# Two neighbouring seven-product pairs in the down projection give way to single ones

## The chip, the cores and the metric

The kernel runs on one core of a Trainium2 chip. The metric is the device time of one execution in microseconds (us). Engines are named as in the profile: PE does matmuls, PEld the weight loads beside them, DVE elementwise work, ACT casts, copies and activations, POOL a few small things, and SP issues the transfers of the weights.

## The reference

One decoder layer on 256 tokens of width 2048, all float32. Cut to what matters here:

```python
h = rmsnorm(x, pre_mlp_g[l])
f = jnp.square(jax.nn.relu(h @ w_up[l])) @ w_down[l]     # 2048 -> 8192 -> 2048
x = x + rmsnorm(f, post_mlp_g[l])
```

Ahead of it stands the token mixing: an input projection, four mixers, and a merge under sigmoid gates whose logits are `z = h @ w_in[l]`. The gate part of that projection (2048 rows, 8192 columns) is computed in the same way as the down projection, and it serves as a comparison below.

## The kernel before

**Three matmuls for one product.** Every float32 matrix is split into a part `hi` of few bits and a remainder `lo`. A product of a 128x128 block of activations with a 128x512 block of weights is three matmuls: hi by hi, hi by lo, lo by hi (lines 808, 809, 810 in `eight_sums`). A weight tile arrives by a 1 MB transfer as `raw`, 128 rows of 2048 numbers (three buffers). `w_emit` takes it in pieces of at most 1024 columns: ACT casts the piece to `hi` (line 102), DVE subtracts to get `lo` (line 103). There are four buffers of `hi` and four of `lo`, so the cast of a piece waits until PE is done with the piece four before it.

**Calls and pairs.** The hidden width of 8192 is worked off in four quarters `q`. In each, the up projection fills `fx` (16 blocks of 128 hidden channels by 256 tokens), and then `eight_sums` multiplies it with w_down: two calls a quarter, one for each half of the output columns, but only one call in the last quarter (its other half goes through `chunk_nat` as tile `dn`). That is seven calls. A call goes through eight pairs `p` of row blocks, 0 to 7. A pair is one `raw` tile: 2x2 blocks of weights against 2x2 blocks of activations.

**Seven or eight products.** A pair outside of `SEVEN` takes eight block products, 24 matmuls, from two pieces of weights. A pair in `SEVEN` takes a scheme with seven, 21 matmuls, at the price of sums and differences on both sides. On the side of the weights `seven(raw)` makes them in place, in four pieces that hang on each other:

```python
def first():      # after the cast and the remainder of piece 1
    V.tensor_tensor(b4[:, :, 0], b4[:, 1], b4[:, :, 0], ALU.subtract)          # line 161
def second():     # after those of piece 2
    V.tensor_tensor(b4[:, 1, 1], b4[:, 1, 1], b4[:, 0, 0], ALU.subtract)       # line 164
    V.tensor_tensor(b4[:, 0, 1], b4[:, 0, 1], b4[:, 1, 1], ALU.subtract)       # line 165
return [(b4[:, 0], first), (b4[:, 1, 1], second), (b4[:, :, 0], None), (b4[:, :, 1], None)]
```

Pieces 1, 3 and 4 have 1024 columns, piece 2 has 512. PE uses the pieces in this order for 6, 3, 6 and 6 matmuls. On the side of the activations, `keep_sums` writes four 128x128 sums for every pair of `SEVEN` into `sx`, during the up projection.

**Results.** Eight PSUM banks M1 to M8 add up over the call. M1, M5, M6 and M7 take products of seven-product pairs alone, so they are complete in the last such pair, which is pair 5. `evac` copies a finished bank to `acc` on ACT in the first quarter (line 1164) and adds it there on DVE in the others (line 1166).

**The gate projection.** It has six calls of the same `eight_sums` with `SEVEN_G = (1, 3, 5)`, on tiles of the same size from w_g, and another evacuation (`evac_g`: M1 and M5 are copied on ACT, sums on DVE follow).

The order of instructions on each engine is fixed when the program is built. It isn't always that of the code: a ready matmul may be put ahead of one whose operand was expected later.

Of the kernel before, what the change touches and what calls it, by code (L numbers as in the profile page):

```python
# [32 lines left out]
QK_SCALE = 192 ** -0.5  # L33
TWO_PI = 6.283185307179586

SEVEN = (1, 2, 4, 5)
SEVEN_G = (1, 3, 5)


# [35 lines left out]
def trunk(ctx: ExitStack, tc: tile.TileContext, t: dict):  # L75
# [16 lines left out]
    def w2(name):  # L92
        return sm.tile([P, 512], F32, tag="w2", name=name, bufs=5)
# [7 lines left out]
    def split(src, hi, lo):  # L101
        a = A.copy(hi, src)  # L102
        return a, V.tensor_tensor(lo, src, hi.bitcast(F32), ALU.subtract)  # L103


    def w_items():
# [30 lines left out]
        for q in range(NQ):  # L137
# [5 lines left out]
            for h in range(2 if q < NQ - 1 else 1):  # L143
                for p in range(8):
                    yield (t["w_down"].rearrange("(r c g) p n -> r g p c n", c=2, g=4)[
                        q * 2 + h, p // 2, :, :, p % 2 * HC:(p % 2 + 1) * HC], PC, "seven" if p in SEVEN else "eight")
            if q == NQ - 1:
# [99 lines left out]
    def small(name, n=1):  # L247
        return cst.tile([P, n], F32, name=name)
# [520 lines left out]
    def sums(ue, uo):  # L769

        s = w2("s")
        s1, s3, s_2, s4 = (s[:, o * P:(o + 1) * P] for o in range(4))
        V.tensor_tensor(s1, ue[:, P:], uo[:, P:], ALU.add)
        V.tensor_tensor(s3, ue[:, :P], ue[:, P:], ALU.subtract)
        V.tensor_tensor(s_2, s1, ue[:, :P], ALU.subtract)
        V.tensor_tensor(s4, uo[:, :P], s_2, ALU.subtract)
        return s

    def eight_sums(xs, sx, which, evac):

        def row(k, i):
            return tuple(xs[:, k, a, i * P:(i + 1) * P] for a in range(2))

        def products():
            for p in range(8):
                a11, a21, a12, a22 = row(2 * p, 0), row(2 * p, 1), row(2 * p + 1, 0), row(2 * p + 1, 1)
                if p in which:
                    u1, u3, u2, u4 = (sx(which.index(p), o) for o in range(4))
                    yield (M1, a11, 0), (M2, a12, 512)
                    yield (M3, u4, 0),  # L790
                    yield (M7, u3, 512), (M5, u1, 0)
                    yield (M4, a22, 0), (M6, u2, 512)
                else:
                    yield (M2, a11, 0), (M2, a12, 512), (M4, a21, 0), (M4, a22, 512)
                    yield (M3, a11, 0), (M3, a12, 512), (M8, a21, 0), (M8, a22, 512)
        pieces = list(products())
        left = [sum(m[0] == b for piece in pieces for m in piece) for b in range(8)]
        ps = [None] * 8
        for piece in pieces:
            hi, lo = w_get()  # L800
            due, late[:] = list(late), []
            for b, (xh, xl), off in piece:
                first = ps[b] is None
                if first:
                    ps[b] = (bank if b < 4 else aux)("sum")
                left[b] -= 1
                wh, wl = hi[:, off:off + 512], lo[:, off:off + 512]
                T.matmul(ps[b], xh, wh, start=first, stop=False)  # L808
                T.matmul(ps[b], xh, wl, start=False, stop=False)  # L809
                T.matmul(ps[b], xl, wh, start=False, stop=not left[b])  # L810
                if not left[b]:
                    late.append(lambda b=b: evac(b, ps))
            for e in due:
                e()
            tick()
# [262 lines left out]
    def keep_sums(p, ue, uo):  # L1078
        i = SEVEN.index(p)
        split(sums(ue, uo), sx[:, i, 0], sx[:, i, 1])  # L1080

    def first_hidden(fx):
# [7 lines left out]
        for c in range(0, 4, 2):  # L1090
# [4 lines left out]
            split(tp.rearrange("p (e s) -> p e s", e=2), fx[:, c:c + 2, 0], fx[:, c:c + 2, 1])  # L1095
            if c // 2 in SEVEN:
                uc = w2("uc")
# [7 lines left out]
    xr = mp.tile([P, NT, D], F32, tag="og", name="xr")  # L1105
    sx = mp.tile([P, len(SEVEN), 2, 512], F32R, tag="xg", name="sx")
    fst = [small(f"fst{i}", 4) for i in range(NT)]
# [30 lines left out]
    for q in range(NQ):  # L1138
# [7 lines left out]
        for b in range(4 if q == 0 else 0, KQ):  # L1146
# [5 lines left out]
            split(u, fx[:, b, 0], fx[:, b, 1])  # L1152
            if b // 2 in SEVEN:
                if b % 2:
# [7 lines left out]
        def evac(h, b, ps):  # L1162
            if q == 0:
                A.copy(acc[h][:, b], ps[b])
            else:
                V.tensor_tensor(acc[h][:, b], ps[b], acc[h][:, b], ALU.add)

        for h in range(2 if q < NQ - 1 else 1):
            eight_sums(fx, lambda i, o: tuple(sx[:, i, a, o * P:(o + 1) * P] for a in range(2)), SEVEN,
                       lambda b, ps, h=h: evac(h, b, ps))  # L1170
# [135 lines left out]
```

## Time and profile before

| what | value |
|---|---|
| median of 3 runs | 1502.41 us (1500.91 to 1505.73) |
| the profiled execution's own time | 1501.62 us |
| its span, first to last instruction | 1499.9 us |
| mean granted TensorE clock | 0.996 |
| PE busy | 1472.8 us (98%) |
| PEld busy | 1236.3 us (82%) |
| DVE busy | 1205.1 us (80%) |
| ACT busy | 800.8 us (53%) |

Busy matmuls overlap each other in this profile (one of 512 columns lasts about 0.39 us, and the next starts before it ends), so the pace of PE is read from starts, not from durations. Rows of the windows give the stretch, its length, the busy time and count of PE, PEld, DVE, ACT and POOL, the granted clock (1.00 is full), the busy share of the DMA engines and GB/s. Rows of the timeline give the start, the duration of the group, and in brackets the idle time of the engine ahead of it.

### The profile page before, as it was taken

The numbers are of one execution on the slowest core, as the hardware profiler recorded it, in microseconds if no ns is written. First come the engines' busy times: TensorE is split into PE (matmuls) and PEld (weight loads), VectorE is DVE, ScalarE is ACT, GpSimd is POOL, SyncE is SP. The second block draws the span as 40 slices with busy tenths as digits, with TensorE's granted clock in tenths as the row PEclk, the third lists the DMA queues.
The fourth block names the chain that finished last, engine by engine and source line by source line (L and its number), as shares of the span: only waits on it lengthen the run. The fifth ranks groups of instructions, "written<-read, shape, count | busy, mean of one in ns | idle before, by whom it ended". The sixth has DMA issues, their size and how long they took to land.

```text
span 1499.9 us, 18735 instructions
## 1 busy us (share of the span) xinstructions
PE 1472.8 (98%) x7192; PEld 1236.3 (82%) x7192; DVE 1205.1 (80%) x1697; ACT 800.8 (53%) x1078; POOL 20.0 (1%) x36
## 2 busy tenths in 40 slices
PE   9999999999999999999999999999999999999997
PEld 7988888888888888888878887888778887788875
DVE  6878788977798798796668888777997779987886
ACT  6655655445555555554445656655554545555552
POOL 0100000000000000000000000000000000000000
PEclk9999999999999999999999999999999999999999
DMA  8655544544655655656656645655556545655563
GB/s 268 219 192 173 180 171 153 187 172 167 226 200 172 226 203 170 226 203 241 245 213 253 216 164 200 213 194 194 169 171 227 194 166 199 210 184 196 168 253 113
DMA packets 57113, 295.76 MB, mean 197 GB/s; under 512 B 5120, under 2 KB 5248, under 8 KB 36544
## 3 DMA queue, kind: packets, MB, share of 16 engines
q1 hardware_dynamic: 55072, 280.68, 53.7%
q0 software_dynamic: 1952, 13.89, 2.6%
q8 instruction: 56, 0.92, 0.2%
q14 instruction: 33, 0.27, 0.1%
HBM read 290.36 MB, written 4.19 MB: 196 GB/s over the span
## 4 chain that ended last, share of the span: by engine, by line
PE 90%; DVE 5%; ACT 2%; issue 1%; DMA 1%; POOL 0%; POOLq 0%; ACTq 0%; SPq 0%; DVEq 0%
PE up L216 15%; PE sum L810 10%; PE sum L809 10%; PE sum L808 10%; PE up L219 8%; PE yb L205 2%; PE yb L206 2%; PE yb L207 2%; ACT hi L102 2%; DVE lo L103 2%; PE zg L205 2%; PE zg L207 2%; PE zg L206 2%; PE o L206 2%; PE o L205 2%; PE o L207 2%
## 5 line engine op out<-in xcount | busy, mean ns | idle before, releaser
L102 ACT CAST hi<-raw 128x1024 fp32r<-128x1024 f32 (+3 forms) x624 | 621.3, 1012 | 461.0 <-PE sum L810 112.3
L103 DVE TENSOR_TENSOR lo<-raw,hi 128x1024 fp32r<-128x1024 f32 (+3 forms) x624 | 720.9, 1173 | 168.3 <-ACT hi L102 160.8
L216 PE MATMUL up<-h,hi 128*128 128x512 f32 x960 | 229.9, 391 | 0.0
L216 PEld LDWEIGHTS up<-h,hi 128*128 128x128 f32 x960 | 176.3, 188 | 34.1
L808 PE MATMUL sum<-hi,fx 128*128 128x512 f32 x308 | 121.6, 395 | 12.3 <-ACT hi L102 12.3
L219 PEld LDWEIGHTS up<-h,lo 128*128 128x128 f32 x960 | 123.1, 191 | 4.7
L219 PE MATMUL up<-h,lo 128*128 128x256 f32 x960 | 124.8, 283 | 0.0
L809 PE MATMUL sum<-lo,hx 128*128 128x512 f32 x312 | 121.4, 389 | 0.0
L810 PE MATMUL sum<-hi,hx 128*128 128x512 f32 x312 | 121.4, 389 | 0.0
L808 PE MATMUL sum<-hi,hx 128*128 128x512 f32 x312 | 121.4, 389 | 0.0
L809 PE MATMUL sum<-lo,fx 128*128 128x512 f32 x308 | 120.0, 390 | 0.0
L810 PE MATMUL sum<-hi,fx 128*128 128x512 f32 x308 | 119.9, 389 | 0.0
L244 ACT COPY jn<-up 128x256 f32<-128x256 f32 x60 | 22.4, 372 | 115.3 <-PE up L216 115.3
L808 PEld LDWEIGHTS sum<-hi,fx 128*128 128x128 f32 x308 | 57.8, 188 | 30.3 <-ACT hi L102 18.4
L245 DVE TENSOR_TENSOR u<-up,jn 128x256 f32<-128x256 f32 x60 | 25.4, 424 | 65.0 <-ACT jn L244 65.0
L809 PEld LDWEIGHTS sum<-lo,hx 128*128 128x128 f32 x312 | 58.6, 188 | 12.3
L810 PEld LDWEIGHTS sum<-hi,hx 128*128 128x128 f32 x312 | 58.6, 188 | 12.2
L808 PEld LDWEIGHTS sum<-hi,hx 128*128 128x128 f32 x312 | 58.6, 188 | 12.2
L810 PEld LDWEIGHTS sum<-hi,fx 128*128 128x128 f32 x308 | 57.8, 188 | 12.3
L809 PEld LDWEIGHTS sum<-lo,fx 128*128 128x128 f32 x308 | 57.8, 188 | 12.2
L161 DVE TENSOR_TENSOR raw<-raw 128x1024 f32<-128x1024 f32 x46 | 56.0, 1218 | 0.2
L500 DVE SCALAR_TENSOR_TENSOR cy<-glu,consts,cy 128x253 f32<-128x253 f32 (+15 forms) x120 | 55.3, 463 | 0.6
(409 smaller groups left out, 2400.1 us busy)
## 6 DMA issues: line engine op xcount, KB each, us to landing
raw<-in_w_g SPq DMA_DIRECT2D x64, 1024.0 KB, 5.5
raw<-in_w_up SPq DMA_DIRECT2D x64, 1024.0 KB, 4.9
raw<-in_w_down SPq DMA_DIRECT2D x64, 1024.0 KB, 5.5
raw<-in_w_out SPq DMA_DIRECT2D x16, 1024.0 KB, 4.9
raw<-in_attn_proj SPq DMA_DIRECT2D x8, 1024.0 KB, 4.9
raw<-in_w_ca SPq DMA_DIRECT2D x4, 1024.0 KB, 4.9
raw<-in_w_cg SPq DMA_DIRECT2D x4, 1024.0 KB, 5.1
raw<-in_w_sv SPq DMA_DIRECT2D x4, 1024.0 KB, 4.8
```

The costliest lines, as they stand in the source:

```text
L102: a = A.copy(hi, src)
L103: return a, V.tensor_tensor(lo, src, hi.bitcast(F32), ALU.subtract)
L161: V.tensor_tensor(b4[:, :, 0], b4[:, 1], b4[:, :, 0], ALU.subtract)
L205: T.matmul(o, xh, wh, start=first, stop=False)
L206: T.matmul(o, xh, wl, start=False, stop=False)
L207: T.matmul(o, xl, wh, start=False, stop=last)
L216: T.matmul(ps, w[0][:, off:off + P], xs[:, k].rearrange("p a s -> p (a s)"), start=first, stop=last)
L219: T.matmul(ps[:, :S], w[1][:, off:off + P], xs[:, k, 0], start=False, stop=False)
L500: V.scalar_tensor_tensor(y, glu[:, b, :S - w], c, y, ALU.mult, ALU.add)
L808: T.matmul(ps[b], xh, wh, start=first, stop=False)
L809: T.matmul(ps[b], xh, wl, start=False, stop=False)
L810: T.matmul(ps[b], xl, wh, start=False, stop=not left[b])
```

## The change

One constant. The pairs of the down projection that take seven products are 1, 3 and 5 instead of 1, 2, 4 and 5. Pairs 2 and 4 then take eight, and pair 3 takes seven. The loader (line 146), the sums of the activations (lines 1096, 1153), the size of `sx` (line 1106) and the products (line 787) all read this constant.

```diff
-SEVEN = (1, 2, 4, 5)
+SEVEN = (1, 3, 5)
 SEVEN_G = (1, 3, 5)
```

## Rows read from the trace of the kernel before

**Rows 1.** The page: busy time, share, instructions of two engines.

```profile
PE 1472.8 (98%) x7192; PEld 1236.3 (82%) x7192; DVE 1205.1 (80%) x1697; ACT 800.8 (53%) x1078; POOL 20.0 (1%) x36
```

**Rows 2.** Waits of PE, whole span: total us, times, longest.

```profile
PE sum L808 <- ACT hi L102: 12.3, 14, 1.2
```

**Rows 3.** Timeline of PE: wait in pair 2, call 1; pair 5, call 3.

```profile
886.68 0.50 PE L808 MATMUL sum<-hi,fx 128*128 128x512 f32 x1 [0.71 <-ACT hi L102]
...
1078.93 0.50 PE L808 MATMUL sum<-hi,fx 128*128 128x512 f32 x1 [1.18 <-ACT hi L102]
```

**Rows 4.** Windows: down calls 1 and 3, gate call 1, an up projection.

```profile
872.90:916.20 43.30, 41.90 (x182) 33.51 (x181) 36.17 (x39) 26.59 (x33) 0.00 (x0) 1.00 0.57 192
...
1048.50:1092.30 43.80, 41.91 (x182) 33.52 (x181) 39.85 (x46) 23.20 (x26) 0.00 (x0) 1.00 0.57 194
...
355.10:396.60 41.50, 41.50 (x184) 34.34 (x184) 37.53 (x42) 23.21 (x26) 0.00 (x0) 1.00 0.58 207
...
959.50:1048.50 89.00, 89.00 (x513) 78.64 (x512) 63.31 (x98) 46.81 (x67) 0.00 (x0) 1.00 0.54 188
```

**Rows 5.** The chain that ended last, 1056 to 1084: start, us, what.

```profile
1071.76 1.06 ACT hi L102
1072.84 1.83 DVE lo L103 x2
1074.67 1.15 DVE raw L161
1075.84 0.69 DVE raw L164
1076.53 0.60 DVE acc L1166
1077.13 0.61 DVE raw L165
1077.84 1.05 ACT hi L102
```

**Rows 6.** Timeline of PE: first and last of six gate calls, and after.

```profile
355.14 0.39 PE L808 MATMUL sum<-hi,hx 128*128 128x512 f32 x1
...
396.65 0.39 PE L205 MATMUL yb<-hi,ox 128*128 128x512 f32 x1
...
636.93 0.39 PE L808 MATMUL sum<-hi,hx 128*128 128x512 f32 x1
...
678.45 0.39 PE L205 MATMUL yb<-hi,px 128*128 128x512 f32 x1
```

**Rows 7.** Timeline of PE: first matmul of the down calls, and after them.

```profile
872.93 0.39 PE L808 MATMUL sum<-hi,fx 128*128 128x512 f32 x1
...
959.43 0.61 PE L216 MATMUL up<-h,hi 128*128 128x512 f32 x2
...
1048.50 0.39 PE L808 MATMUL sum<-hi,fx 128*128 128x512 f32 x1
...
1136.04 0.62 PE L216 MATMUL up<-h,hi 128*128 128x512 f32 x2
...
1225.11 0.39 PE L808 MATMUL sum<-hi,fx 128*128 128x512 f32 x1
...
1312.62 0.62 PE L216 MATMUL up<-h,hi 128*128 128x512 f32 x2
...
1401.69 0.39 PE L808 MATMUL sum<-hi,fx 128*128 128x512 f32 x1
...
1445.42 0.39 PE L205 MATMUL dn<-hi,fx 128*128 128x512 f32 x1
```

**Rows 8.** Timeline of ACT, DVE and PE: pair 5 of gate call 2.

```profile
440.16 1.05 ACT L102 CAST hi<-raw 128x1024 fp32r<-128x1024 f32 x1 [1.36 <-PE sum L810]
...
441.25 1.23 DVE L103 TENSOR_TENSOR lo<-raw,hi 128x1024 fp32r<-128x1024 f32 x1 [1.02 <-ACT hi L102]
...
443.32 0.39 PE L808 MATMUL sum<-hi,hx 128*128 128x512 f32 x1
```

## The prediction

> **What bounds the kernel now.** I read the page first. PE is busy 98% of the span and DVE 80% [rows 1]: no engine but PE can be the bound on the whole, and only some 27 us of PE's span (1499.9 less 1472.8) are idle. What a lighter DVE is worth must therefore show as idle time of PE, in the stage that the change touches. So I asked for PE's waits next. One line stands out: matmuls of line 808 waited 14 times for a cast of ACT, 12.3 us in all [rows 2]. Fourteen is twice seven, and the down projection has seven calls. The timeline of PE puts two of these waits in each call, the first where pair 2 and the second where pair 5 is worked off, the second of two neighbours each time [rows 3]. There is none at pair 1 or 4, the first neighbours, which come behind a pair with eight products.
>
> The windows by call say that this is the whole of it: a down call leaves PE idle for 1.4 to 1.9 us, the gate call and the up projection for nothing, all at full clock [rows 4]. The chain that ended last runs through ACT and DVE just ahead of these waits: cast of piece 1, two remainders, the difference of line 161, those of 164 and 165, and the cast of piece 4, for which PE waits [rows 5].
>
> **Why neighbours wait.** Piece 1 of pair 5 may be cast when PE is done with the piece four before it, piece 1 of pair 4. From there PE has 15 matmuls of pair 4 and 15 of pair 5 until it wants piece 4. At the pace of the gate call, 41.51 us for 183 matmuls or 0.2268 us each [rows 6], that is 6.8 us; as far as 6 less (5.4 us) if the program has put piece 4's first matmul ahead of those of piece 3, which the waiting matmul hints at. The chain from the start of the first cast to the end of the last takes 1071.76 to 1078.89, or 7.1 us [rows 5]. So the wait must lie between 0.3 and 1.7 us, and 1.18 was measured [rows 3].
>
> **The change, part by part.**
>
> *Products added.* Each call gets one more (61 instead of 60), three matmuls. Seven calls: 21 matmuls at 0.2268 us, +4.76 us on PE, which nothing hides.
>
> *Waits removed.* The calls last 86.50 us (two, first quarter), 87.54, 87.51 and 43.73 us [rows 7], 305.28 us in all for 7 x 180 = 1260 matmuls. At the gate's pace these would take 285.8 us. The excess is 19.5 us: the 12.3 us of idle time, and some 7 us in which PE starts late but counts as busy, since its modelled durations overlap. By call, 43.25 us in the first quarter is 2.42 over the 40.83 that 180 matmuls need, or 1.21 for each wait; later calls are 2.9 over, so their second wait costs 1.7. With pairs 1, 3 and 5 no seven-product pair stands behind another. Does a single one wait? The gate call answers: the same function, pieces and triple of pairs, the same 1 MB tiles, and its first and its sixth call last 41.51 and 41.52 us [rows 6]. I take this row as the price of a changed call: 7 x 41.51 = 290.6 us, against 305.3. That is -14.7 us, the +4.76 included.
>
> *Does the gate call stand for a down call?* It differs in the evacuation. M1 is complete with the first piece of pair 5. In quarters 1 to 3 (five calls) the bank is added on DVE, between the differences, where it holds the chain up for 0.60 us [rows 5]; the gate copies it on ACT. It explains why the later second waits are 0.47 us longer (1.18 against 0.71) [rows 3]. What room has a single pair 5? Its piece 1 gets the buffer of pair 3's piece 3, from which PE has 6 + 24 + 15 = 45 matmuls, 10.2 us, until piece 4: 3 us more than the chain of 7.1 us, which holds the add already. Piece 4 itself can be cast only when pair 4 is done. In the gate call that cast starts at 440.16, the remainder ends at 442.48, and the matmul that reads it is the second of piece 4, at 443.32 + 0.23 = 443.55 [rows 8]. The spare is 1.07 us, and an add of 0.6 to 0.7 fits into it. So I take nothing for it. The bound from above is that pair 5 keeps its present wait in these five calls: 5 x 1.7 = 8.6 us.
>
> *DVE and ACT work removed.* Each call loses one scheme of seven: a cast and a remainder of 1024 columns and one of 512, and lines 161, 164 and 165 once. With 1.23 us for a remainder of 1024 columns [rows 8], that is about 4.4 us of DVE a call (1.2 + 0.6 for remainders, 1.2 + 0.7 + 0.7 for the differences). DVE goes from 39.9 busy us to about 35.5 in 41.5, under the gate's 37.5 [rows 4]. It is worth nothing beyond the waits above.
>
> *Sums of the activations.* Three instead of four in each quarter, on DVE and ACT in the up projection. There PE is busy 89.00 of 89.00 us and DVE 63.31 [rows 4]: PE covers it before and after. Worth nothing; if that cover were gone, it would be a gain.
>
> *Transfers.* The same 8 MB a call (8.39 million bytes), in less time: 202 GB/s against 194 now. The gate call moves 207 GB/s through the same three buffers with PE never idle [rows 4]. Worth nothing. No instruction moves to another queue, and what the waits hold up today is PE alone; next late would be the first bank of the following call, whose evacuation is as before.
>
> **Weighed against a rule.** The wait repeats at the same places, twice a call [rows 2, 3]. The Trainium skill, page "Perfetto Trace Analysis", section "Identifying Performance Opportunities", says that a gap repeating on the engine that should be saturated can mean too little buffer space for the next tile. Four buffers of `hi` are left as they are; if that alone decided, all waits would stay and the time would be that of the rival "waits stay" below. The trace bears the rule out only in part: the gate call has the same four buffers and no gap [rows 6], because the four pieces ahead of a single pair hold more matmuls.
>
> **The sum.** 1501.62 us (the profiled execution's own time, 0.8 under the median of the three runs) - 14.7 = 1486.9 us. I say 1487.
>
> **The rivals.**
>
> *A pair 5 that still waits.* The DVE add comes between the differences, and the fixed order may put piece 4 early again. For: it lengthens the wait today by 0.47 us [rows 3]. Against: 3 us of room, and 1.07 in the tightest place. It costs from 5 x 0.47 = 2.4 to 8.6 us: 1489 to 1496 us.
>
> *The waits stay.* Their length is set by the chain and the four buffers, not by the neighbour; then the 21 matmuls come on top: 1501.6 + 4.8 = 1506.4 us. Against: pairs 1 and 4 don't wait now, nor do the gate's.
>
> *Every single pair waits* (the other side at its worst). If a 7.1 us chain were too long behind an eight-product pair as well, since there pieces of 12 matmuls hold the buffers longer, three pairs a call would wait 1.21 us or more instead of two: 7 x 1.21 = 8.5, and 4.8 for the products: about 1515 us. It decides from 0.70 us a pair on (14.7 us over 21 pairs); below that the change is still a gain. Against it are the same rows.
>
> *Half of the gain lost elsewhere* (DMA late by the faster pace, or another order of DVE at the ends of calls): 7 us less, 1494 us. In the gate rows nothing speaks for it.
>
> **How the numbers follow.** A measurement of this kernel tells about 0.3%, 4.5 us, from no change. All waits gone, 1485.5 to 1489 us: 0.82. Pair 5 still waits or part is lost, 1489 to 1497: 0.12. Between 1497 and 1506: 0.03. The waits stay or grow, 1506 to 1515: 0.03. The likeliest gives 1487. The range goes from 1485 (the other run-to-run side, as 1500.91 stands to 1501.62, and a little of late start at the ends of calls) to 1492, which takes in the larger part of the second case. Faster by more than 0.3%: 0.94; within 0.3%: 0.03; slower: 0.03.
>
> **What the changed profile would show.** The line of 14 waits of line 808 for the cast is gone. A down call lasts 41.5 us in each quarter, and none shows PE idle. Line 161 counts seven fewer, the matmuls of `sum` 21 more. The up projections still take 89.07 us from call to call. It would be wrong if a call lasts more than 42 us, first of all at pair 5 of quarters 1 to 3, or if a wait of the kind PE for DVE's `lo` comes in its place.

## The result and the profile after

The changed kernel takes 1487.68 us, the median of four runs (1487.48 to 1488.71), against 1502.88 us before (1500.91 to 1505.73). The ratio is 0.9899, with a 95% interval of 0.9882 to 0.9916. The profiled execution took 1487.72 us, its span is 1486.0 us. The prediction said 1487 us, 1485 to 1492.

First the waits of PE over the whole span, from the changed kernel (total us, times, longest). It is the full answer:

```profile
PE zq L205 <- ACT hi L102: 2.1, 3, 1.2
PE idle L283 <- DVE ones L279: 1.1, 1, 1.1
PE zq L206 <- DVE lo L103: 0.5, 1, 0.5
PE tph L1014 <- DVE hn L1009: 0.2, 1, 0.2
PE o L206 <- DVE lo L103: 0.2, 1, 0.2
```

The line that led [rows 2], 14 waits of line 808 for the cast, 12.3 us, is gone, and no other line of the down projection (tile `sum`) took its place. Line 161 runs 39 times, 46 before. The windows, with the columns of [rows 4]: first the two calls of quarter 0, then those of quarter 1, then the up projection between:

```profile
873.40:914.90 41.50, 41.50 (x184) 34.34 (x183) 32.14 (x35) 25.45 (x31) 0.00 (x0) 1.00 0.59 203
914.90:956.50 41.60, 41.60 (x184) 34.38 (x184) 31.99 (x31) 25.25 (x30) 0.00 (x0) 1.00 0.57 206
1045.60:1087.10 41.50, 41.50 (x184) 34.34 (x183) 35.57 (x41) 22.27 (x24) 0.00 (x0) 1.00 0.60 205
1087.10:1128.70 41.60, 41.60 (x184) 34.37 (x184) 36.45 (x40) 21.61 (x22) 0.00 (x0) 1.00 0.59 204
956.60:1045.50 88.90, 88.90 (x513) 78.59 (x512) 61.97 (x93) 46.17 (x66) 0.00 (x0) 1.00 0.55 187
```

PE is busy for the whole of every window, and DVE has fallen from 39.85 to 35.57 us in call 3. The starts of the calls, and of what follows them, in the timeline of PE:

```profile
873.40 0.39 PE L808 MATMUL sum<-hi,fx 128*128 128x512 f32 x1
...
956.52 0.39 PE L216 MATMUL up<-h,hi 128*128 128x512 f32 x1
...
1045.59 0.39 PE L808 MATMUL sum<-hi,fx 128*128 128x512 f32 x1
...
1128.70 0.39 PE L216 MATMUL up<-h,hi 128*128 128x512 f32 x1
...
1217.77 0.39 PE L808 MATMUL sum<-hi,fx 128*128 128x512 f32 x1
...
1300.89 0.39 PE L216 MATMUL up<-h,hi 128*128 128x512 f32 x1
...
1389.96 0.39 PE L808 MATMUL sum<-hi,fx 128*128 128x512 f32 x1
...
1431.52 0.39 PE L205 MATMUL dn<-hi,fx 128*128 128x512 f32 x1
```

Against [rows 7]: 83.12 us for two calls in each of the first three quarters and 41.56 for the single call of the last, 290.92 in all from starts before rounding, where 305.28 stood. That is 14.4 us less. The span fell by 13.9; the missing 0.5 is already there before the first call (873.40 against 872.93), ahead of the place that the change aims at.

### The profile page after: what moved, and what is told of

Read it like the earlier page. It is cut to its first block, busy times and chain, and to the rows that moved or that the text cites. A ratio compares the mean times of both kernels' runs of the same rounds, so it can differ in the third digit from the quotient of the medians.

```text
span 1486.0 us, 18686 instructions
## 1 busy us (share of the span) xinstructions
PE 1471.0 (99%) x7213; PEld 1241.9 (84%) x7213; DVE 1171.1 (79%) x1642; ACT 792.1 (53%) x1060; POOL 20.0 (1%) x36
## 4 chain that ended last, share of the span: by engine, by line
PE 95%; DMA 2%; issue 1%; DVE 1%; POOL 0%; ACT 0%; SPq 0%; POOLq 0%; DVEq 0%; ACTq 0%
PE up L216 15%; PE sum L809 12%; PE sum L808 12%; PE sum L810 12%; PE up L219 8%; PE yb L205 2%; PE yb L206 2%; PE yb L207 2%; PE zg L207 2%; PE zg L205 2%; PE zg L206 2%; PE o L206 1%; PE o L207 1%; PE o L205 1%; DMA xg<-in_x 1%; PE hd L216 1%
## 5 line engine op out<-in xcount | busy, mean ns | idle before, releaser
L102 ACT CAST hi<-raw 128x1024 fp32r<-128x1024 f32 (+3 forms) x610 | 614.8, 1017 | 457.8 <-PE sum L810 145.5
L103 DVE TENSOR_TENSOR lo<-raw,hi 128x1024 fp32r<-128x1024 f32 (+3 forms) x610 | 708.6, 1179 | 180.7 <-ACT hi L102 173.3
L808 PE MATMUL sum<-hi,fx 128*128 128x512 f32 x343 | 133.4, 389 | 0.0
L809 PE MATMUL sum<-lo,fx 128*128 128x512 f32 x343 | 133.4, 389 | 0.0
L810 PE MATMUL sum<-hi,fx 128*128 128x512 f32 x343 | 133.4, 389 | 0.0
L808 PEld LDWEIGHTS sum<-hi,fx 128*128 128x128 f32 x343 | 64.4, 188 | 13.5
L810 PEld LDWEIGHTS sum<-hi,fx 128*128 128x128 f32 x343 | 64.4, 188 | 13.4
L809 PEld LDWEIGHTS sum<-lo,fx 128*128 128x128 f32 x343 | 64.4, 188 | 13.4
L808 PEld LDWEIGHTS sum<-hi,hx 128*128 128x128 f32 x312 | 58.6, 188 | 12.3
L809 PEld LDWEIGHTS sum<-lo,hx 128*128 128x128 f32 x312 | 58.6, 188 | 12.3
L205 PE MATMUL zg<-hi,hx 128*128 128x512 f32 x128 | 51.5, 403 | 0.0
```

The source lines that it names most:

```text
L205: T.matmul(o, xh, wh, start=first, stop=False)
```

## Experiments

Two theories ran against each other. *Neighbour theory*: PE waits where a seven-product pair stands directly behind another, because the chain of its four pieces then doesn't fit between the release of its first buffer and the use of its last piece. *Load theory*: PE waits because DVE has too much to do in a call with four such pairs. The change takes away both the neighbours and the load, so its own time can't tell them apart. Each ratio is to the kernel before, run in the same session: 1502.64 us for the first four experiments, 1502.58 for the next four, 1503.12 for the last four. Lengths of calls are taken from the starts of their matmuls in the timeline of PE, as in [rows 7].

**Two neighbours, three pairs.**

```diff
-SEVEN = (1, 3, 5)
+SEVEN = (1, 2, 5)
```

> Pairs 1, 2 and 5 take seven products: three as in the changed kernel, two of them neighbours as in the kernel before. Neighbour theory (a seven-product pair waits only when another stands directly before it): pair 2 waits in every call, pair 5 does not, so 7 waits of PE for the cast of about 1.2 us each, and 1487.7 + 8.5 = about 1496 us. Load theory (the number of seven-product pairs in a call, that is DVE's load, sets the waits): no waits, about 1488 us.

1496.9 us (ratio to before 0.9959, 0.9945 to 0.9974). The waits of PE:

```profile
PE sum L808 <- ACT hi L102: 5.0, 7, 0.7
```

Seven, one a call, at pair 2. Its calls last 42.75 us against 41.56: a wait costs 1.19 us with what lies around it, where the prediction had 1.21. Call 3 in the windows:

```profile
1048.20:1091.00 42.80, 42.09 (x185) 34.25 (x184) 35.72 (x41) 21.85 (x24) 0.00 (x0) 1.00 0.58 198
```

DVE's load is that of the changed kernel (35.72 us against 35.57), and yet PE waits: the calls are 8.3 us longer in all, and the median is 9.2 us higher.

**Four single pairs.**

```diff
-SEVEN = (1, 3, 5)
+SEVEN = (0, 2, 4, 6)
```

> Four seven-product pairs a call as in the kernel before, none of them neighbours. Neighbour theory: no waits, each call 180 matmuls at 0.2271 us = 40.9 us, 7 x 0.68 = 4.8 us under the changed kernel, about 1483 us. Load theory: DVE does the work of the kernel before, so PE waits again, about 1500 us.

1485.52 us (0.9886, 0.9871 to 0.9900): no wait in the down projection, with as many seven-product pairs as before. It missed the expected 1483 us: the calls take 288.13 us, where seven of 40.9 would take 286.3. It is the fastest pair list of the first four runs, and was run again at the end, where its calls are looked at.

**Two single pairs**, `SEVEN = (2, 5)`.

> Two single seven-product pairs a call, so one block product more than the changed kernel (62). It prices that product alone: both theories say no waits and 7 x 0.68 = 4.8 us over the changed kernel, about 1492.5 us. If the lighter DVE were worth something by itself, the time would lie under that.

1492.67 us (0.9933, 0.9919 to 0.9948), no wait. The seven calls take 295.49 us, 4.6 over the changed kernel: the price of seven products, 21 matmuls. Relieving DVE further is worth nothing.

**Six buffers instead of four**, for the kernel before:

```diff
+        more[:1] = [m + 1 for m in more[:1]]
+        if more and more[0] % 3 == 2:
+            both = more[1].tile([P, D], F32R, tag="rg", name="both", bufs=2)
+            hi, lo = both[:, :HC], both[:, HC:]
+        else:
...                                      # hi and lo as before
```

The code is cut: `more` counts the pieces from the first up projection to the end of the last quarter. Each third piece goes into a tile `both`, its two halves serving as `hi` and `lo`; there are two such tiles, in the buffers of the row gains. Line numbers are higher by 6 from there on (815 is the old 809).

> The kernel before (pairs 1, 2, 4, 5), but from the up projection of the first quarter on six buffers of hi and of lo instead of four (each third piece goes into the buffers of the row gains, which are free there). Neighbour theory with the buffers as its cause: the first piece of pair 5 can then be cast when PE is done with the first piece of pair 3, 48 matmuls or 10.9 us ahead of piece 4 instead of 6.8, more than the chain of 7.1; the waits are gone or under 0.4 us each, 1483 to 1488 us. Load theory: DVE's work is unchanged, the 14 waits stay, about 1502 us.

1488.55 us (0.9902, 0.9886 to 0.9919). With pairs 1, 2, 4 and 5 left in place, 14 us come back. Waits of the down projection, and windows: the two calls of quarter 1, then the second call of quarter 2.

```profile
PE sum L815 <- DVE both L103: 1.2, 1, 1.2
...
PE sum L815 <- DVE lo L103: 0.8, 1, 0.8
```

```profile
1045.60:1087.00 41.40, 41.40 (x182) 33.76 (x181) 37.17 (x41) 22.30 (x26) 0.00 (x0) 1.00 0.60 199
1087.00:1129.40 42.40, 41.64 (x181) 33.64 (x180) 40.36 (x46) 23.17 (x25) 0.00 (x0) 1.00 0.58 195
...
1259.60:1302.50 42.90, 41.72 (x181) 33.56 (x180) 40.77 (x46) 23.65 (x25) 0.00 (x0) 1.00 0.58 197
```

None of the 14 waits for the cast is left. Two waits for a remainder of DVE stand in the two calls where DVE is busy 40.36 of 42.40 and 40.77 of 42.90 us. So nearly all of what a neighbour costs here needs the four buffers; whether the last two waits come from the amount of DVE's work was not tried. The lower end of what was expected, 1483 us, wasn't reached; PE's pace was slower too (last section).

**A single pair last in the call**, `SEVEN = (1, 3, 5, 7)`.

> Four single pairs again, but the last pair of a call is one of them, so that all eight banks are complete only in pair 7. Neighbour theory: no waits for the cast, 1483 us at best. A rival for the place: the eight evacuations now fall on the end of the call together, and the next call's first products want the banks M2 and M4 while DVE or ACT still adds them, 1 to 2 us at each of the calls' ends, 1487 to 1493 us.

1487.87 us (0.9898, 0.9883 to 0.9913). There are two waits of about 1 us, one each in the second call of quarters 1 and 2:

```profile
1097.21 0.50 PE L808 MATMUL sum<-hi,fx 128*128 128x512 f32 x1 [1.03 <-ACT hi L102]
```

It is for a cast, 9.2 us into that call, at pair 1, a single pair. No matmul waits for a bank, as the rival had it, though the time lies in the rival's range. The timeline of DVE shows what stands in the chain of that pair:

```profile
1091.19 1.22 DVE L161 TENSOR_TENSOR raw<-raw 128x1024 f32<-128x1024 f32 x1
1092.32 0.68 DVE L1166 TENSOR_TENSOR acc<-sum,acc 128x512 f32<-128x512 f32 x1
...
1093.52 0.68 DVE L1166 TENSOR_TENSOR acc<-sum,acc 128x512 f32<-128x512 f32 x1
...
1094.72 0.69 DVE L1166 TENSOR_TENSOR acc<-sum,acc 128x512 f32<-128x512 f32 x1
1095.32 0.68 DVE L165 TENSOR_TENSOR raw<-raw 128x512 f32<-128x512 f32 x1
```

Three adds of the call before stand between its operations (161, the remainder of piece 2, 164, 165), 0.6 us from each to the next operation, and DVE never pauses there. So a pair needs no neighbour to be late; work of another kind inside its chain does it too. No run took these adds away.

**A shorter chain.** The kernel before without line 165, in both projections (a difference on one block of weights is left out):

```diff
-            V.tensor_tensor(b4[:, 0, 1], b4[:, 0, 1], b4[:, 1, 1], ALU.subtract)
```

> The kernel before without the second difference of second() (line 165), in both projections: one block of weights is left without its difference, so this part of the computation is left out. The chain from the first cast to the last is 0.6 to 0.7 us shorter. Neighbour theory: each of the 14 waits gets shorter by as much, those in the first quarter and at pair 2 nearly vanish as idle time, 14 x 0.7 = 9.8 us, about 1493 us. Buffers alone (the wait is set by the number of buffers, not by the length of the chain): about 1502 us.

1494.21 us (0.9944, 0.9927 to 0.9961). The 14 waits are still 14, but 3.0 us in all instead of 12.3, and the calls take 296.19 us, 9.1 less. The length of the chain sets the wait, as the prediction's sum of the chain had it.

**A longer chain.** The changed kernel with

```diff
-            V.tensor_tensor(b4[:, 0, 1], b4[:, 0, 1], b4[:, 1, 1], ALU.subtract)
+            for op in (ALU.subtract, ALU.add, ALU.subtract)[:3 if down else 1]: V.tensor_tensor(b4[:, 0, 1], b4[:, 0, 1], b4[:, 1, 1], op)
```

The list `down` is filled ahead of the first up projection, so the gate projection keeps one operation. The three operations together leave the same block as one.

> The changed kernel, but in the down projection line 165 runs three times (subtract, add, subtract), so the chain of every seven-product pair is 1.2 us longer and DVE does 3.6 us more in a call. It tests the room that the prediction gave a single pair: 10.2 us (8.8 with the matmul put ahead) against a chain of 7.1, now 8.3. If the room is there, the time stays at 1488 us. If a single pair was at its edge, 21 pairs wait by up to 1.2 us: up to 1513 us.

1504.87 us (1.0014, 1.0005 to 1.0024). This fell out against the prediction's room of 3 us: two short operations of DVE in each of three pairs undid the whole gain. The seven calls take 306.03 us, 15.1 over the changed kernel, and the waits for the cast are back:

```profile
PE sum L808 <- ACT hi L102: 6.5, 15, 0.8
```

The timeline of DVE at pair 3 of the first call, and a window of that call:

```profile
887.15 0.69 DVE L164 TENSOR_TENSOR raw<-raw 128x512 f32<-128x512 f32 x1
887.88 0.69 DVE L165 TENSOR_TENSOR raw<-raw 128x512 f32<-128x512 f32 x1
888.49 1.22 DVE L103 TENSOR_TENSOR lo<-raw,hi 128x1024 fp32r<-128x1024 f32 x1
889.63 1.41 DVE L165 TENSOR_TENSOR raw<-raw 128x512 f32<-128x512 f32 x2
892.22 2.36 DVE L103 TENSOR_TENSOR lo<-raw,hi 128x1024 fp32r<-128x1024 f32 x2 [1.19 <-ACT hi L102]
```

```profile
873.30:916.40 43.10, 42.40 (x183) 33.88 (x183) 35.35 (x40) 24.85 (x31) 0.00 (x0) 1.00 0.55 189
```

The remainder of piece 3 (the line at 888.49) has slipped in between the differences. From the end of the first line 165 to that of the last it is 2.5 us instead of 1.4. Piece 4's cast then waits for the last of them, and DVE stands idle for 1.19 us in the very pair that makes PE late. DVE's 35.35 us in this window are less than the changed kernel's 35.57 in call 3, which has no wait: so it isn't the amount of DVE's work that makes PE wait here.

**Six buffers and single pairs**, 0, 2, 4 and 6.

> Single pairs 0, 2, 4, 6 and six buffers of hi and lo from the first quarter of the up projection on. If buffers are what the remaining starts of 0.1 us of the pairs 0, 2, 4, 6 lack, each call takes 40.9 us and the time is 1483 us. If DVE is full instead (about 40 us of work in a call of 40.9), the buffers change nothing, 1485 us.

1485.79 us (0.9888, 0.9873 to 0.9903). No wait in the down projection and no late start, but calls of 41.4 to 41.5 us, not of 40.9. Nothing is gained over four buffers, and the reason is neither of the two expected; see the last section.

**One operation longer**, line 165 twice in the down projection (the list of the longer chain cut to two subtractions, so that one block of weights carries a difference too many).

> The changed kernel with line 165 run twice in the down projection (a second subtraction, so one block of weights is wrong by one difference): 0.69 us more in the chain instead of the two operations (1.4 us) of e7. The tightest place of a single pair had 1.07 us to spare in the gate call. If that spare is right, 0.69 us fits, the waits stay away and the time is that of the changed kernel, 1488 us. If a single pair has no room, about half of what e7 lost comes back, 1494 to 1497 us.

1490.39 us (0.9917, 0.9902 to 0.9932), between the two: the seven calls take 293.59 us, 2.7 over the changed kernel. Timelines of DVE and of PE, at pair 5 of call 3:

```profile
1071.46 0.69 DVE L165 TENSOR_TENSOR raw<-raw 128x512 f32<-128x512 f32 x1
1072.07 1.22 DVE L103 TENSOR_TENSOR lo<-raw,hi 128x1024 fp32r<-128x1024 f32 x1
1073.20 0.68 DVE L165 TENSOR_TENSOR raw<-raw 128x512 f32<-128x512 f32 x1
1073.81 0.68 DVE L1167 TENSOR_TENSOR acc<-sum,acc 128x512 f32<-128x512 f32 x1
1075.08 2.36 DVE L103 TENSOR_TENSOR lo<-raw,hi 128x1024 fp32r<-128x1024 f32 x2 [0.59 <-ACT hi L102]
```

```profile
1075.89 0.39 PE L808 MATMUL sum<-hi,fx 128*128 128x512 f32 x1
1076.36 0.50 PE L809 MATMUL sum<-lo,fx 128*128 128x512 f32 x1
```

Here PE is late at the place that the prediction had called the tightest: the remainder of piece 4 ends at 1075.08 + 1.22 = 1076.30, and the second matmul of piece 4 was due at 1075.89 + 0.23 = 1076.12. It started at 1076.36. (Line 1167 is the old 1166.) The same start is late in all seven calls; pairs 1 and 3 don't wait.

**Less load, outside of the chain.** The kernel before with

```diff
-                V.tensor_tensor(acc[h][:, b], ps[b], acc[h][:, b], ALU.add)
+                if b in (M1, M5, M6, M7):
+                    V.tensor_tensor(acc[h][:, b], ps[b], acc[h][:, b], ALU.add)
```

> The kernel before without the adds of the banks M2, M4, M3 and M8 in quarters 1 to 3 (only the first quarter's sums are kept for these four, so part of the computation is left out). They run at the end of a call, outside of the chain of pairs 2 and 5. DVE loses 4 x 0.68 = 2.7 us in five calls, more than half of the 4.4 us that the change takes from it. Neighbour theory: the 14 waits stay as they are, 1502 us. Load theory: a lighter DVE shortens them, 1494 us or less.

1502.8 us (0.9999, 0.9990 to 1.0009). Its waits and windows of quarter 1:

```profile
PE sum L808 <- ACT hi L102: 12.3, 14, 1.2
```

```profile
1050.20:1093.90 43.70, 41.80 (x181) 33.44 (x180) 38.46 (x44) 23.20 (x26) 0.00 (x0) 1.00 0.57 192
1093.90:1137.70 43.80, 41.90 (x182) 33.48 (x181) 38.32 (x40) 22.53 (x24) 0.00 (x0) 1.00 0.58 195
```

The second call of that quarter before, for comparison:

```profile
1092.30:1136.00 43.70, 41.80 (x181) 33.43 (x180) 40.52 (x45) 22.51 (x24) 0.00 (x0) 1.00 0.57 193
```

DVE has 1.4 us less to do in the first of these calls (39.85 in [rows 4]) and 2.2 us less in the second, and the waits are those of before to the tenth. It is less relief than the 2.7 us expected: in the second call of quarter 2 only 0.2 us are gone.

**The changed kernel and the four single pairs, side by side.**

> The changed kernel once more, beside the next run: 1487.7 us.

> Pairs 0, 2, 4, 6 once more, beside the changed kernel. Neighbour theory: 21 matmuls less than the changed kernel and no waits for the cast, less the 0.9 us that the second calls of quarters 1 and 2 lost in e2: about 3 us under the changed kernel, 1485 us. Load theory: the same as the changed kernel or slower.

1489.23 us (0.9907, 0.9890 to 0.9923) and 1484.52 us (0.9881, 0.9867 to 0.9896). Windows of the two calls of quarter 1 of the latter:

```profile
1043.40:1084.30 40.90, 40.90 (x181) 33.81 (x180) 37.37 (x41) 23.63 (x26) 0.00 (x0) 1.00 0.61 203
1084.30:1126.10 41.80, 41.79 (x181) 33.39 (x180) 40.31 (x45) 23.16 (x24) 0.00 (x0) 1.00 0.61 206
```

DVE is busy 40.31 of 41.80 us in the second call, and PE shows no wait; in the experiment before this one, 38.46 of 43.70 us went with two waits. So DVE's load is not what makes the 14 waits. It isn't free either: the second call lasts 0.9 us longer than the first, because some of its first matmuls start 0.1 to 0.2 us late without idle time of PE in the profile. With six buffers these late starts are gone.

The calls take 288.17 us against 290.92, 2.75 less. The two profiled executions are 5.87 us apart (1489.98 and 1484.11); the other 3.1 us arise ahead of the first call, which started at 875.63 in one and at 872.52 in the other. That start belongs to the run rather than to the pair list: in the earlier profiles of the same two kernels it was 873.40 and 875.05. Pairs 0, 2, 4 and 6 are the better version of the two, by 2 to 3 us.

## Why the prediction was right

**The bound and the place.** The waits at pairs 2 and 5, with the late starts around them, were what the calls had to give. They are gone, and the up projection takes 89.07 us from call to call as before.

**The products.** 4.76 us were set for 21 matmuls. The run with pairs 2 and 5 alone measured 4.6 for as many.

**The waits.** The price of a changed call was read from the gate call, 41.51 us; it is 41.56 in all seven. So 290.6 us were said and 290.9 measured, and 1486.9 against 1487.72 in the profiled execution. That the whole time came out within 1 us is in part luck: the same kernel, run again, took 1489.23 us with calls of the same length. The reading of 1.21 us for a wait is confirmed with 1.19 by the list 1, 2, 5. That neighbours make the waits is shown by the lists 1, 2, 5 and 0, 2, 4, 6, that the length of the chain sets them by the run without line 165, that load does not by the list 1, 2, 5, the run without the late adds and the list 0, 2, 4, 6.

**The add on DVE at pair 5** was priced at nothing. The timelines of ACT, DVE and PE of the changed kernel, pair 5 of call 3:

```profile
1071.72 1.05 ACT L102 CAST hi<-raw 128x1024 fp32r<-128x1024 f32 x1 [1.39 <-PE sum L810]
```

```profile
1069.93 0.69 DVE L165 TENSOR_TENSOR raw<-raw 128x512 f32<-128x512 f32 x1
1070.54 1.22 DVE L103 TENSOR_TENSOR lo<-raw,hi 128x1024 fp32r<-128x1024 f32 x1
1072.36 0.69 DVE L1166 TENSOR_TENSOR acc<-sum,acc 128x512 f32<-128x512 f32 x1 [0.60 <-PE sum L810]
1072.96 2.42 DVE L103 TENSOR_TENSOR lo<-raw,hi 128x1024 fp32r<-128x1024 f32 x2
```

```profile
1075.12 0.39 PE L809 MATMUL sum<-lo,fx 128*128 128x512 f32 x1
```

The add no longer stands between the differences but behind them and the remainder of piece 3, and most of it runs while DVE would wait for the cast of piece 4. The remainder of piece 4 ends at 1072.96 + 1.22 = 1074.18, and 0.94 us are left until the matmul that reads it; the gate's 1.07 were nearly the right size.

**Where a step was off.** "3 us more than the chain" is not the room that a single pair has. It is the tightest place that counts, for which the prediction had 1.07 us. And the sum counted the chain as if DVE did nothing else. DVE takes its instructions in one fixed order, and an operation more in the chain comes with another order: in the run with one operation longer the remainder of piece 3 (1072.07) stands between the two runs of line 165, where in the changed kernel it stands behind the only one (1070.54). With 0.69 us more, the remainder of piece 4 came 1.1 us later (1076.30 against 1074.18, less the 0.99 by which that call began later), past the 0.94 of room; with 1.4 us more the gain was gone. The change won its time with 0.94 us to spare at that place.

**The rule weighed.** The Trainium skill, page "Perfetto Trace Analysis", section "Identifying Performance Opportunities", says that a gap that repeats can mean too little buffer space. The prediction held that the trace bears it out only in part. The run with six buffers bears it out more: with neighbours left as they were, none of the 14 waits for the cast remains, and two waits for a remainder, 2.0 us in all against 12.3, take their place. For the waits of this kernel, four buffers and neighbours are needed together, and removing either takes away all or nearly all of them. It holds for a chain of this length: with the longer chains, single pairs were late too.

## What to carry to other kernels

Where the same function runs twice in a kernel with different settings, the stage without waits is a measured price for the other: here it was 41.51 us said and 41.56 measured for a call. When an engine's work comes in bursts, look at where the bursts stand before looking at how much there is of them: here 40.3 us of DVE in a call came with no wait and 0.9 us of late starts, and 38.5 us with two waits, in a call that lasted 2.9 us more than its matmuls need. And a chain's room has to be read from the rows at its last link (when the operand is ready, when it is wanted), since an operation more can change the order of everything beside it.

## What the runs showed that was not expected

In the two kernels that put each third piece into the buffers of the row gains, matmuls followed each other more slowly without any gap: with pairs 0, 2, 4 and 6 the first two calls took 82.92 us for 360 matmuls, 0.2303 us each, against 81.81 us or 0.2273 with four buffers. It takes back 1.1 us in two calls, more than the 0.9 us of late starts that six buffers remove in quarters 1 and 2. The three up projections between the calls went the other way: 88.72, 88.67 and 88.64 us from call to call, where the other kernels took 89.07. Whether the place of the buffers or both halves lying in one tile makes either was not tried.
